# Output projection, first half: a third pair of k tiles by seven block products, and another order of the k tiles

## The chip, the cores and the metric

The kernel runs on one core of a Trainium2 chip. The engines of a core work side by side, each through its own instructions in order: TensorE (PE; its weight loads are listed as PEld), VectorE (DVE), ScalarE (ACT), GpSimd (POOL), and SyncE (SP), which issues most DMAs. The metric is the device time of one execution in microseconds (us); of several runs the median is given.

## The reference

One layer of an encoder block on 256 tokens of width 2048, in float32. Only the output projection is touched. A state-space mixer gives 1024 columns, a pooling mixer the other 1024; they are joined and multiplied by one matrix:

```python
y_ssd = ssd_mixer(z, xbc, dt_raw, ...)
y_pool = pool_mixer(u, pool_w[i], pool_scale[i])
mix = jnp.concatenate([y_ssd, y_pool], axis=-1) @ w_out[i]
h = h + rmsnorm(mix, mix_norm_post[i])
```

`w_out` has 2048 x 2048 elements. A gated feed-forward layer and a per-layer embedding follow.

## The kernel before

**Precision.** Every float32 operand is split into a rounded high part (`hi`, cast by ACT) and the rest (`lo`, a subtraction on DVE), and a product is three matmuls: high by high, high by rest, rest by high. `split` (line 146) does this to weights, in tiles of the tag "w", of which there are five (`weight_pair`, line 142). Raw weights come by DMA into tiles of the tag "raw", of which there are three.

**The projection.** The 2048 input features are 16 k tiles of 128: tiles 0 to 7 are the state-space mixer's, 8 to 15 the pooling mixer's. The output columns are made in two halves of 1024. `sublayer` (line 874) calls `token_major` (line 330) for each half; it runs through the k tiles in pairs, eight steps, in the order of a list. A half has four accumulators in PSUM, `acc[t][n]`: two blocks of 128 tokens by two blocks of 512 columns. An ordinary step casts and splits two weight tiles of 1024 columns and issues 2 x 2 x 2 x 3 = 24 matmuls of 128x512.

**Seven products.** A step in `fast` takes its two k tiles as a 2 x 2 block product with seven multiplications in place of eight (`seven_products`, line 277): 7 x 3 = 21 matmuls. For it

- the weights are split in four parts: a (one block of 512 columns), b, d and c (two blocks each). a and b are blocks of the raw weights, d and c blocks of sums that `add_blocks` (line 270, four DVE additions of 128x512) makes. For the tile pairs 0 and 2 of both halves these sums were made early in the kernel and stored in DRAM (`early_add`), and are loaded again; for other pairs `add_blocks` writes them over the raw tile, after a and b were split from it;
- the activations need sums too: `Sums` (line 853) makes them (one DVE addition of 128x512, four of 128x128, a cast on ACT and a subtraction on DVE) the first time that a pair is asked for, and keeps them for the other half;
- four of the seven products have accumulators of their own (`alt`: two main banks and the two banks of the tag "misc"), the other three go to `acc`. The order of the products is a11 (part a), a12 (b), a22 (d), s4 (b), s2 (d), s1 (c), s3 (c).

After the last fast step, `combine` (line 308, one copy on ACT and eight DVE operations of 128x512) adds the four into `acc`. It is issued with the step that follows, whose matmuls go column by column; in the last step of a half they do so too.

In the first half, the list is 8, ..., 15, 0, ..., 7; steps 4 and 5 (counted from 0: tiles 0, 1 and 2, 3) are fast, step 6 (tiles 4, 5) has the combination and step 7 (tiles 6, 7) is the last. In the second half the pairs 12, 0 and 2 are fast, as steps 2, 3 and 4; the sums of the activations of 12 and the block sums of its weights are made there.

**The turns.** Tiles 0 to 7 are the state-space mixer's output y, transposed by PE in `y_turn` (line 823, eight transposes and two scaled copies, on ACT and DVE, for two tiles). A list of jobs (line 831) puts these turns behind the ordinary steps 0 to 3: none, 0, then 2 and 4, then 6. A fast step runs no jobs.

**After a half**, each accumulator is read by ACT (a square with its sum) and by DVE (a product with the gain), lines 897 and 898. The banks of the first half's `acc` and `alt` are those of the second half's.

The order of the engines' work around here is a scheduler's: it takes it from the program's order, from what is ready in its own model, and from the tiles that are free.

Of the kernel before, what the change touches and what calls it, by code (L numbers as in the profile page):

```python
# [38 lines left out]
V_MIX, V_SCW, V_SCB, V_SN, V_PS, V_FN = 0, 16, 76, 88, 96, 104  # L39
# [14 lines left out]
def build(nc, a, out):  # L54
    x = a["x"][0]

    w_dtu, w_xbc, w_z, w_out, w_up = a["w_dtu"], a["w_xbc"], a["w_z"], a["w_out_"], a["w_up"]
# [3 lines left out]
    with tile.TileContext(nc) as tc, \  # L61
# [12 lines left out]
        def page(name, dtype=F32):  # L74
            return gp.tile([P, 2048], dtype, tag="pg", bufs=13, name=name)
# [4 lines left out]
        def tiny(name, n=2):  # L80
            return sp.tile([P, n], F32, tag="tiny", bufs=40, name=name)

        def main(name):
            return [pm.tile([P, 512], F32, tag="main", name=f"{name}_{i}") for i in range(2)]
# [32 lines left out]
        def load(dst, src, ahead=False):  # L117

            with tc.issue_after(last["dma"]) if last and not ahead else nullcontext():
                return ins(nc.sync.dma_start(dst, src))  # L120
# [15 lines left out]
        def vec(i):  # L136
            return xt[0][:, i:i + 1] if i < V_SCW else vt[:, i - V_SCW:i - V_SCW + 1]
# [53 lines left out]
        def put(dst, src, scale):  # L191

            hi, lo = dst
            return (ins(nc.scalar.activation(hi, src, AF.Identity, scale=scale)),
                    ins(nc.vector.scalar_tensor_tensor(lo, src, scale, hi.bitcast(F32),  # L195
                                                       op0=ALU.mult, op1=ALU.subtract)))
# [3 lines left out]
        work = []  # L200
# [204 lines left out]
        def rms(name, parts, scale, n=1):  # L405

            base = EPS
            for i, q in enumerate(parts):
                m = tiny(f"{name}m{i}", n)
                nc.gpsimd.tensor_scalar(m, q, scale, base, op0=ALU.mult, op1=ALU.add)  # L410
                base = m
            r = tiny(f"{name}r", n)
            nc.gpsimd.tensor_tensor(r, m, mhalf[:, :n], op=ALU.pow)
            return r

        def panel_part(name, pan, src, vcol, k0, k1):

            first = None
            for k in range(k0, k1, 2):
                ps = misc(f"{name}t{k}")  # L420
                for j in range(2):
                    for t in range(2):
                        nc.tensor.transpose(ps[:, (2 * j + t) * P:(2 * j + t + 1) * P],
                                            src[t][:, (k + j) * P:(k + j + 1) * P], ident)
                for j in range(2):
                    done = put(pan(k + j), ps[:, j * L:(j + 1) * L], vec(vcol + k + j))
                    first = first or done
            return first
# [212 lines left out]
        cat = Panel.__new__(Panel)  # L641
# [106 lines left out]
        def job(f, *args):  # L748
            return lambda: f(*args)
# [73 lines left out]
        def y_turn(k):  # L823
# [4 lines left out]
                                        y[:, t * 1024 + (k + j) * P:t * 1024 + (k + j + 1) * P], ident)  # L828
            for j in range(2):
                put(cat(k + j), ps[:, j * L:(j + 1) * L], vec(V_SN + k + j))  # L830
        work.extend([[], [job(y_turn, 0)], [job(y_turn, 2), job(y_turn, 4)], [job(y_turn, 6)]])

        def gload(name, src):
            g = cp.tile([P, D], F32, tag="gain", name=name)
            load(g, src.partition_broadcast(P))
            return g
# [37 lines left out]
        def sublayer(name, w, ks, get, gain, h, vnext, panel=Panel, fast=((), ()), sums=None, at=(), row=None, then=()):  # L874

            mg = []
            sq = [[], []]
            for half in range(2):

                alt = main(f"{name}s{half}") if fast[half] and half == 0 else []  # L880
                acc = [main(f"{name}a{half}{t}") for t in range(2)]
                if fast[half]:
                    alt += main(f"{name}s{half}") if half else []
                token_major(f"{name}{half}", w, half * 1024, ks[half], get, acc, 1, fast[half], alt, sums, at if half else ())
                mg.append(page(f"{name}m{half}"))
                for t in range(2):
                    for n in range(2):
                        q = tiny(f"{name}q{t}{half}{n}", 1)
                        m = mg[half][:, t * 1024 + n * 512:t * 1024 + (n + 1) * 512]
                        junk = sp.tile([P, 512], F32, tag="junk", bufs=1, name=f"{name}j{t}{half}{n}")  # L890
                        c = slice(half * 1024 + n * 512, half * 1024 + (n + 1) * 512)
                        b = acc[t][n]
                        if row:
                            nc.scalar.activation(junk, b, AF.Square, scale=row[t], accum_out=q)
                            nc.vector.scalar_tensor_tensor(m, b, row[t], gain[:, c], op0=ALU.mult, op1=ALU.mult)
                        else:
                            nc.scalar.activation(junk, b, AF.Square, accum_out=q)
                            nc.vector.tensor_mul(m, b, gain[:, c])
                        sq[t].append(q)
            r = [rms(f"{name}{t}", sq[t], 1.0 / D) for t in range(2)]  # L900
            pan = panel(f"{name}x")
            for c in range(4):
                s = slice(c * 512, (c + 1) * 512)
                for t in range(2):
                    m = mg[c // 2][:, t * 1024 + c % 2 * 512:t * 1024 + (c % 2 + 1) * 512]
                    nc.vector.scalar_tensor_tensor(h[t][:, s], m, r[t], h[t][:, s],
                                                   op0=ALU.mult, op1=ALU.add)
                panel_part(f"{name}x", pan, h, vnext, 4 * c, 4 * c + 4)
                if c in then:
                    then[c]()  # L910
            return pan
# [15 lines left out]
        h = [page(f"h{t}") for t in range(2)]  # L927
        for t in range(2):
            load(h[t], x[t * P:(t + 1) * P, :])
        hf = sublayer("wo", w_out, (list(range(8, 16)) + list(range(8)), [8,9,10,11,12,13,0,1,2,3,14,15,4,5,6,7]), cat, gload("gmix", a["mix_norm_post"][0]), h,  # L930
                      V_FN, Pairs, ((4,5),(2,3,4)), Sums("cs", cat))


        pl = [ple(0)]
# [415 lines left out]
```

## Time and profile before

| | us |
|---|---|
| median of three runs | 1105.33 (1105.0 to 1105.36) |
| the profiled execution | 1104.6 |
| its span, first to last instruction | 1102.8 |
| output projection, first half, on PE | 195.84 to 240.81 |
| second half, on PE | 240.81 to 283.3 |

The span is the time from the first to the last instruction of the profiled execution; 1.8 us lie around it. A row of a timeline has the start in us, how long the instruction (or a row of like ones, with their count x) took, the engine, the line of the code, the operation, the tile written <- the tiles read, shapes, and in brackets how long the engine had been idle and what released it. A matmul's row lasts longer than its turn, since matmuls overlap; its cost is the distance from start to next start. The same goes, in a smaller measure, for DVE and ACT. In the names, digits of steps are left out in places: `wo_0w` is the first weight tile of an ordinary step, `wo02dw` part d of the pair 2 of half 0, `wo112aw` part a of the pair 12 of half 1, `css` and `csp` the sums of activations, `cath` and `catl` the activations' high part and rest, `yt` the turn of y, `wom` what the last product with the gain writes.

### The profile page before, as it was taken

The numbers are of one execution on the slowest core, as the hardware profiler recorded it, in microseconds if no ns is written. First come the engines' busy times: TensorE is split into PE (matmuls) and PEld (weight loads), VectorE is DVE, ScalarE is ACT, GpSimd is POOL, SyncE is SP. The second block draws the span as 40 slices with busy tenths as digits, with TensorE's granted clock in tenths as the row PEclk, the third lists the DMA queues.
The fourth block names the chain that finished last, engine by engine and source line by source line (L and its number), as shares of the span: only waits on it lengthen the run. The fifth ranks groups of instructions, "written<-read, shape, count | busy, mean of one in ns | idle before, by whom it ended". The sixth has DMA issues, their size and how long they took to land.

```text
span 1102.8 us, 16019 instructions
## 1 busy us (share of the span) xinstructions
PE 1094.5 (99%) x5946; PEld 946.5 (86%) x5946; DVE 977.1 (89%) x1372; ACT 729.0 (66%) x1067; POOL 86.5 (8%) x145
## 2 busy tenths in 40 slices
PE   9999999999999999999999999999999999999997
PEld 9999988888888888888888888888888888888886
DVE  6589998898868998889889988898999999999996
ACT  6958763566775665665756646657688878776773
POOL 0210000100100000000000000000000000051001
PEclk9999999999999999999999999999999999999998
DMA  9885248556489999989999998999999999996872
GB/s 364 358 343 191 101 180 369 209 198 240 163 362 389 390 421 357 406 340 371 382 367 381 367 390 347 400 365 422 367 409 375 368 347 395 416 379 225 315 272 76
DMA packets 57246, 361.69 MB, mean 328 GB/s; under 512 B 6352, under 2 KB 7504, under 8 KB 21200
## 3 DMA queue, kind: packets, MB, share of 16 engines
q1 hardware_dynamic: 45648, 298.71, 69.1%
q0 software_dynamic: 11088, 61.35, 14.5%
q8 instruction: 46, 0.75, 0.3%
q10 hardware_dynamic: 432, 0.62, 0.2%
q14 instruction: 32, 0.26, 0.1%
HBM read 306.65 MB, written 54.00 MB: 327 GB/s over the span
## 4 chain that ended last, share of the span: by engine, by line
PE 97%; ACT 1%; DVE 1%; issue 0%; POOL 0%; POOLq 0%
PE ga L90 22%; PE va L90 22%; PE dna L90 11%; PE woa L90 7%; PE xbc L90 5%; PE gt L90 5%; PE dns L90 4%; PE z L90 4%; PE dtu L90 4%; PE dn0s L90 2%; PE dn1s L90 2%; PE ple L90 1%; PE gts L90 1%; PE wos L90 1%; PE yd L90 1%; PE pw L90 1%
## 5 line engine op out<-in xcount | busy, mean ns | idle before, releaser
L90 PE MATMUL ga<-wox,ug_0w 128*128 128x512 f32 x704 | 130.8, 337 | 0.0
L90 PE MATMUL ga<-wox,ug_1w 128*128 128x512 f32 x704 | 130.2, 337 | 0.0
L90 PE MATMUL va<-wox,uv_1w 128*128 128x512 f32 x704 | 129.2, 336 | 0.0
L90 PE MATMUL va<-wox,uv_0w 128*128 128x512 f32 x704 | 129.2, 336 | 0.0
L90 PEld LDWEIGHTS ga<-wox,ug_0w 128*128 128x128 f32 x704 | 107.6, 188 | 14.6 <-ACT pl L919 0.2
L90 PEld LDWEIGHTS ga<-wox,ug_1w 128*128 128x128 f32 x704 | 107.5, 188 | 14.5 <-DVE wox L195 0.2
L90 PEld LDWEIGHTS va<-wox,uv_0w 128*128 128x128 f32 x704 | 107.5, 188 | 14.5
L90 PEld LDWEIGHTS va<-wox,uv_1w 128*128 128x128 f32 x704 | 107.5, 188 | 14.5
L275 DVE TENSOR_TENSOR dnb<-dnb 128x512 f32<-128x512 f32 x128 | 88.3, 690 | 3.0
L250 POOL DMA_DIRECT2D dns<-dnb x30 | 16.1, 536 | 319.4 <-DVE dnb L275 279.8
L90 PE MATMUL xbc<-hnh,xb_0w 128*128 128x256 f32 x192 | 37.9, 284 | 0.1
L90 PE MATMUL xbc<-hnh,xb_1w 128*128 128x256 f32 x192 | 37.1, 283 | 0.0
L846 ACT CAST he<-he 128x512 fp32r<-128x512 f32 x13 | 8.1, 621 | 42.7 <-DVE he L845 42.7
L988 ACT CAST hs<-hid 128x384 fp32r<-128x384 f32 (+1 forms) x44 | 23.4, 536 | 13.5 <-PE dna L90 13.2
L90 PEld LDWEIGHTS xbc<-hnh,xb_0w 128*128 128x128 f32 x192 | 30.8, 189 | 0.8 <-ACT u L571 0.3
L1068 ACT ACTIVATE fc<-gr,vt 128x256 f32<-128x256 f32 x44 | 26.1, 594 | 7.2 <-DVE gr L1061 7.2
L90 PEld LDWEIGHTS xbc<-hnh,xb_1w 128*128 128x128 f32 x192 | 30.7, 189 | 0.1
L90 PE MATMUL dna<-dn_0w,hs 128*128 128x512 f32 x108 | 28.8, 395 | 0.0
L90 PE MATMUL dna<-dn_1w,hs 128*128 128x512 f32 x108 | 28.3, 392 | 0.0
L1139 POOL DMA_DIRECT2D hd<-hsum x24 | 12.9, 539 | 192.6 <-PE dn0s L90 70.4
L989 DVE TENSOR_TENSOR hs<-hid,hs 128x384 fp32r<-128x384 f32 (+1 forms) x44 | 25.5, 584 | 2.4 <-ACT hs L988 2.4
L90 PE MATMUL xbc<-hnl,xb_1w 128*128 128x256 f32 x96 | 27.3, 284 | 0.0
(1779 smaller groups left out, 2870.2 us busy)
## 6 DMA issues: line engine op xcount, KB each, us to landing
dnb<-w_down SPq DMA_DIRECT2D x32, 1024.0 KB, 10.0
dns<-dnb POOLq DMA_DIRECT2D x30, 1024.0 KB, 6.4
hd<-hsum POOLq DMA_DIRECT2D x24, 512.0 KB, 8.4
zr<-w_z SPq DMA_DIRECT2D x8, 1024.0 KB, 4.8
dtur<-w_dtu SPq DMA_DIRECT2D x14, 528.0 KB, 8.7
hsum<-he POOLq DMA_DIRECT2D x13, 512.0 KB, 8.0
wo0r<-w_out_ SPq DMA_DIRECT2D x6, 1024.0 KB, 5.9
gtb<-w_gate SPq DMA_DIRECT2D x6, 1024.0 KB, 10.1
```

The lines of the kernel that those rows point to most:

```text
L90: last["pe"] = ins(nc.tensor.matmul(o, lhsT, rhs, start=start, stop=stop, skip_group_check=True))
L250: nc.gpsimd.dma_start(t, pg[0])
L275: nc.vector.tensor_add(s[:, i], v[:, i], a[:, b])
L846: nc.scalar.copy(o[:, :512], s[:, :512])
L988: nc.scalar.copy(t[:, :c1], hid_part(k)[:, :c1])
L989: nc.vector.tensor_sub(t[:, 512:512 + c1], hid_part(k)[:, :c1], t[:, :c1].bitcast(F32))
L1068: nc.scalar.activation(c[:, f], v[:, f], AF.Identity, bias=vec(V_FCB + 4 * s + 2 * i + f), scale=vec(w + NF))
L1139: nc.gpsimd.dma_start(o.bitcast(F32), kept[k])
```

## The change

Two lists and one set are altered; no function is.

```diff
-        work.extend([[], [job(y_turn, 0)], [job(y_turn, 2), job(y_turn, 4)], [job(y_turn, 6)]])
+        work.extend([[], [job(y_turn, 4)], [job(y_turn, 0), job(y_turn, 2)], [job(y_turn, 6)]])
...
-        hf = sublayer("wo", w_out, (list(range(8, 16)) + list(range(8)), [8,9,10,11,12,13,0,1,2,3,14,15,4,5,6,7]), cat, gload("gmix", a["mix_norm_post"][0]), h,
-                      V_FN, Pairs, ((4,5),(2,3,4)), Sums("cs", cat))
+        hf = sublayer("wo", w_out, ([8,9,10,11,14,15,4,5,0,1,2,3,12,13,6,7], [8,9,10,11,12,13,0,1,2,3,14,15,4,5,6,7]), cat, gload("gmix", a["mix_norm_post"][0]), h,
+                      V_FN, Pairs, ((4,5,6),(2,3,4)), Sums("cs", cat))
```

In the first half, the pairs now come as 8, 10, 14, 4, 0, 2, 12, 6. Steps 4, 5 and 6 (pairs 0, 2 and 12) are fast. The block sums of the weights of pair 12 were not stored for this half, so `add_blocks` makes them in the raw tile. The sums of its activations are asked for first in this half and found again in the second. The combination is issued with step 7, which is also the last of the half. The turn of tiles 4 and 5 comes behind step 1, those of 0 to 3 behind step 2.

## The prediction

> **What bounds the kernel now.** I read the page's busy shares and its chain first, then the chain and the waits of the output projection, then the timelines of the engines there.
>
> ```profile
> PE 1094.5 (99%) x5946; PEld 946.5 (86%) x5946; DVE 977.1 (89%) x1372; ACT 729.0 (66%) x1067; POOL 86.5 (8%) x145
> PE 97%; ACT 1%; DVE 1%; issue 0%; POOL 0%; POOLq 0%
> ...
> 204.70:243.40 38.70, 38.70 (x177) 31.48 (x176) 35.92 (x53) 24.44 (x37) 0.56 (x3) 1.00 0.60 230
> 224.70:229.60 4.90, 4.90 (x22) 3.94 (x21) 4.90 (x6) 4.53 (x6) 0.00 (x0) 1.00 0.57 207
> ```
>
> TensorE (PE) is on 97% of the chain that ended last, so an added or removed microsecond of PE time in this stage is one of the kernel. The two last rows are stretches of the first half (columns: PE, PEld, VectorE (DVE), ScalarE (ACT), GpSimd (POOL) busy, granted clock, DMA): PE is busy in all of the 38.7 us, but DVE is busy in 35.92 of them, and in all 4.90 us of the second block product. The DVE time that the change adds meets a full queue; ACT and DMA (60%) have room.
>
> ```profile
> 212.96 1.03 PE L827 MATMUL yt<-ident,y 128*128 128x128 f32 x8
> 224.71 0.63 PE L90 MATMUL wos<-wo02aw,cath 128*128 128x512 f32 x2
> 225.18 0.39 PE L90 MATMUL wos<-wo02aw,catl 128*128 128x512 f32 x1
> 226.81 0.86 PE L90 MATMUL woa<-wo02bw,csp 128*128 128x512 f32 x3
> 229.61 0.63 PE L90 MATMUL woa<-wo_0w,cath 128*128 128x512 f32 x2
> 235.21 0.63 PE L90 MATMUL woa<-wo_0w,cath 128*128 128x512 f32 x2
> 240.81 1.08 PE L90 MATMUL woa<-wo_0w,cath 128*128 128x512 f32 x4
> ```
>
> These are starts on PE: the pair of tiles 2 and 3 by seven products begins at 224.71, the seventh step (an ordinary pair, 24 matmuls) at 229.61, the eighth at 235.21, the second half at 240.81. An ordinary step takes 5.60 us, so a matmul 0.2333 us; 21 of them take 4.90.
>
> **The change, part by part.** *Removed from PE.* In the seventh step 24 matmuls become 21: 3 x 0.2333 = 0.70 us. PE does not pause anywhere in this stage (the starts follow each other at that pace), so this is the whole possible gain: **-0.70**.
>
> *Added and moved on DVE.* The seventh step takes tiles 12 and 13. The block sums of their weights were not stored ahead, so they are made in place in the raw tile. Of before, the second half does just this with the same tiles (wo112):
>
> ```profile
> 243.33 0.68 DVE L867 TENSOR_TENSOR css<-cath,catl 128x512 f32<-128x512 f32 x1
> 243.93 0.69 DVE L158 TENSOR_TENSOR wo112aw<-wo112r,wo112aw 128x512 fp32r<-128x512 f32 x1
> ...
> 246.48 1.41 DVE L275 TENSOR_TENSOR wo112r<-wo112r 128x512 f32<-128x512 f32 x2
> 247.81 0.68 DVE L847 TENSOR_TENSOR csp<-css,csp 128x512 fp32r<-128x512 f32 x1
> 248.41 1.41 DVE L275 TENSOR_TENSOR wo112r<-wo112r 128x512 f32<-128x512 f32 x2
> 250.99 1.23 DVE L158 TENSOR_TENSOR wo112dw<-wo112r,wo112dw 128x1024 fp32r<-128x1024 f32 x1 [1.17 <-ACT wo112dw L157]
> 252.14 1.22 DVE L158 TENSOR_TENSOR wo112cw<-wo112r,wo112cw 128x1024 fp32r<-128x1024 f32 x1
> ```
>
> ```profile
> 249.91 1.05 ACT L157 CAST wo112dw<-wo112r 128x1024 fp32r<-128x1024 f32 x1 [2.69 <-DVE wo112r L275]
> ```
>
> From start to next start, 512 columns cost DVE 0.60 us (css) and a split of 1024 1.14 (252.14 - 250.99, rounded); the four block adds (L275) cost 1.33 + 1.41 = 2.74. Seven products split 512 + 3 x 1024 columns (4.02 us), an ordinary pair 2 x 1024 (2.28). Added: 4.02 - 2.28 + 2.74 = **4.5 us of DVE**. The sums of the activations (css, csp: 0.6 + 4 x 0.2 + 0.6 = 2.1 us with small gaps) were made for these tiles in the second half; they now come before the seventh step and are found there later. That moves 2.1 us and adds none. ACT gets 1536 more columns to cast (1.6 us by 1.05 for 1024), which lies in its idle time (24.44 of 38.70 busy). DMA: the tile of 12 was loaded whole before and still is; the transfers of stored sums stay. SP issues as many loads.
>
> *The chain in the step.* The parts a and b must be split before their blocks are overwritten; then come the four adds, ACT's cast of d, DVE's rest of d. The third product (a22) needs d: it begins 6 matmuls into the step, and its second matmul, the first to read the rest, one more: 7 x 0.2333 = 1.63 us, at 229.61 + 1.63 = 231.24. In the second half this chain was done early: d at 252.22 with the step beginning at 251.90, so 1.3 us ahead. There ordinary steps, which take two weight tiles each, come ahead of it; here two steps of four tiles do, and there are five tiles:
>
> ```profile
> 224.95 1.05 ACT L157 CAST wo_0w<-wo0r 128x1024 fp32r<-128x1024 f32 x1
> ...
> 227.71 1.05 ACT L157 CAST wo_0w<-wo0r 128x1024 fp32r<-128x1024 f32 x1 [0.27 <-PE woa L90]
> ```
>
> ```profile
> 225.07 1.22 DVE L158 TENSOR_TENSOR wo02cw<-wo02t,wo02cw 128x1024 fp32r<-128x1024 f32 x1
> ```
>
> ACT's first cast for the seventh step starts at 224.95, as the first block product ends (224.71). The cast at 227.71 waited for PE: s4 of the second block product, the last reader of its b, started its three matmuls at 226.81. So tile number n waits for number n - 5. By this, a of tile 12 is cast from 224.95 and b, which waits for the a of the second block product (its last matmul is the one of 225.18, its turn over at 225.41), from about 225.6 to 226.65.
>
> *Lower end:* DVE free, b's rest until 227.9, adds until 230.6, cast of d until 231.75, rest of d until 233.0: PE waits 233.0 - 231.24 = 1.75 us. Were two adds done while ACT casts b, about 0.65 less: 1.1.
>
> *Upper end:* DVE not free. Before, the last split of the second block product began at 225.07, so DVE was through at 226.21. The change delays it, since the turn of y's tiles 0 and 1 moves behind the third step:
>
> ```profile
> 210.02 0.69 DVE L867 TENSOR_TENSOR css<-cath,catl 128x512 f32<-128x512 f32 x1
> ...
> 214.10 1.95 DVE L195 SCALAR_TENSOR_TENSOR catl<-yt,vt,cath 128x256 fp32r<-128x256 f32 x4 [0.60 <-ACT cath L194]
> ...
> 223.93 1.22 DVE L158 TENSOR_TENSOR wo02dw<-wo02t,wo02dw 128x1024 fp32r<-128x1024 f32 x1 [0.46 <-ACT wo02dw L157]
> ```
>
> The sums of tiles 0 and 1 ran from 210.02; now they can't before their turn at 212.96, so 2.1 us of DVE work moves behind 214, into a row whose one gap is that 0.46: the end of these splits moves to 226.21 + 2.1 - 0.5 = 227.8. Then a (0.60) and b (1.14) until 229.5, adds (2.74) until 232.3, cast of d until 233.4, rest of d until 234.6: PE waits 234.6 - 231.24 = **3.4 us**. This takes it that the sums of tiles 12 and 13, whose inputs are ready long before, fill the hole that opens at 210 to 214. I take the middle of 1.75 and 3.4, **2.5 us**, as PE can bring s4 (three matmuls of b, 0.70 us) forward, and DVE some adds.
>
> Behind the waiting a22 stand PE's 14 other matmuls of the step and the whole eighth step, so nothing covers this. Behind the rest of d on DVE stand c and the eighth step's splits; c is needed 2.1 us after a22 starts over and takes 1.14, so no second wait.
>
> *The combination* (8 DVE operations of 0.6) follows the eighth step now; before, it ran under the seventh and eighth, and the read-out needed only the last matmuls:
>
> ```profile
> 237.53 0.69 DVE L898 TENSOR_TENSOR wom<-woa,gmix 128x512 f32<-128x512 f32 x1 [0.49 <-ACT woj L897]
> ```
>
> The eighth step goes column by column, so each part is combined and read out (ACT then DVE, about 1.4 us) as its six matmuls end, 1.4 us apart. The second half's first matmuls go to banks of products that are read early; its seventh matmul, 1.4 us after its start, needs the first read-out, which should be 2 us ahead of it. DVE's work from the eighth step's start until then is 4.8 + 1.2 + 1.1 = 7.1 us in about 7.0: bounds 0 and 1 us, I take 0 since only the two first read-outs must be done. In the second half DVE then lacks the 2.1 us of sums, so it catches up.
>
> *The turns.* Tiles 4 and 5 are turned a step earlier than they were; they need y's last scaling, and have it:
>
> ```profile
> 204.75 0.88 DVE L820 TENSOR_SCALAR y<-y,yn1r 128x512 f32<-128x512 f32 x2 [1.38 <-POOL yn1r L817]
> 206.97 0.60 PE L827 MATMUL yt<-ident,y 128*128 128x128 f32 x4
> ```
>
> 205.63 against 206.97: nothing. There are as many transposes, and this turn lies a whole step (5.60) ahead of the fourth step, which reads it.
>
> **Sum:** -0.70 + 2.5 = **+1.8 us**. Against the profiled execution (1104.6 with a span of 1102.8) that is 1106.4. The median of the runs, 1105.33, is 0.7 above that execution, so my time is 1105.33 + 1.8 = **1107.1**.
>
> **The rivals.** (1) *The sums of 12 do not fill the hole.* They stand behind those of 2 in the program; if DVE takes them there, 2.1 us more stand ahead of a22's weights, of which the 1.1 us of waiting for ACT's cast can hide half: waits of 4.5 to 5.5, so +3.8 to +4.8, about **1109.5**, slower. It decides where css of tile 12 stands: before 214 or after 217. For it, before, DVE idled for 1.38 us ahead of 204.75 and did not take these sums there; against it: there they stood some 40 us further on (243.33), here under 20.
> (2) *No wait.* The weights' chain is taken out of PE's way, by another order of PE's or DVE's work: -0.7, **1104.6**. For it: work of different steps does mix on PE; transposes of the next norm stand amid the ple products:
>
> ```profile
> 286.58 0.38 PE L423 MATMUL woxt<-ident,h 128*128 128x128 f32 x2
> 286.72 0.48 PE L90 MATMUL ple<-ple_0w,ptl 128*128 128x512 f32 x1
> ```
>
> Against it: DVE has no free time before, and the five tiles hold the splits back.
>
> (3) *The clock falls in the wait.* The only pause at the end:
>
> ```profile
> 1094.00:1096.00 2.00, 0.75 (x2) 0.00 (x0) 0.85 (x2) 0.97 (x3) 1.21 (x3) 1.00 0.00 0
> 1096.00:1098.00 2.00, 1.36 (x2) 0.30 (x2) 1.81 (x4) 0.40 (x1) 0.15 (x1) 0.82 0.19 65
> 1098.00:1100.00 2.00, 0.12 (x1) 0.00 (x0) 0.39 (x1) 0.59 (x1) 0.00 (x0) 0.50 0.92 324
> ```
>
> The granted clock (third column from the end) is 1.00 until 1096, 0.82 over the next 2 us and 0.50 then: it fell about 1097.3, some 2.5 us after the last dense matmuls (1094.75). A wait of that size could halve the clock. No row shows how soon it comes back: nothing lost, or, with the 5.5 us of half clock at the end as the nearest row, 2.75; with the forecast up to +4.6, **1109.9**.
> [...]
> (4) *Something else moves:* an order of work elsewhere, by over 2.2 us either way.
>
> **Chances.** About 0.2% (2.2 us) is what a measurement tells from no change. Forecast, waits of 1.1 to 3.4, +0.4 to +2.7: 0.50, of it 0.08 over 2.2. Rival 1: 0.22; 2: 0.17; 3: 0.06; 4: 0.05 (0.03 faster, 0.02 slower). Slower 0.08 + 0.22 + 0.06 + 0.02 = 0.38, same 0.42 + 0.17 = 0.59, faster 0.03. The range takes in rival 2 below and most of rival 1 above: 1104.5 to 1109.8; the likeliest case alone: 1105.7 to 1108.0.
>
> **What would show it.** Right: a pause of PE after the second product of tiles 12 and 13, released by DVE's rest of d or ACT's cast; DVE without gaps from 214 until then; css of tile 12 before 214; the second half beginning 1.8 us later. Wrong: the seventh step 4.9 us long without a pause (rival 2); a longer pause with these sums in front of it (1); a clock under 1.00 there (3); a wait at the second half's start (the combination priced too low).

## The result, and the profile after

| | before | after |
|---|---|---|
| median of five runs, us | 1105.33 (1104.91 to 1105.96) | 1111.13 (1110.33 to 1111.99) |
| ratio, with its 95% interval | | 1.0051 (1.0040 to 1.0062) |
| the profiled execution, us | 1104.6, span 1102.8 | 1111.13, span 1109.4 |
| output projection on PE, us | 195.84 to 283.31: 87.47 | 196.39 to 289.08: 92.69 |

The change made the kernel slower by 5.8 us, three times the 1.8 that was forecast, and past the upper end of the range. The spans differ by 6.6 us: 5.22 of them lie between the first matmul of the projection and the first one behind it, 0.55 ahead of it and 0.8 behind, each less than the 1.05 between the fastest and the slowest run of before. So the 5.22 us are to be found.

The page of after, busy times and the chain that ended last:

```profile
PE 1097.9 (99%) x5943; PEld 947.4 (85%) x5943; DVE 981.3 (88%) x1378; ACT 729.5 (66%) x1069; POOL 84.3 (8%) x145
...
PE 95%; DVE 2%; ACT 1%; DMA 1%; issue 1%; POOL 0%; POOLq 0%; DVEq 0%; ACTq 0%; SPq 0%
```

PE has the three matmuls less (5943 against 5946) and is busy 3.4 us longer; that alone says that its matmuls went slower somewhere. By the rows below, 1.87 of it lie in the projection (89.34 against 87.47 us busy). DVE's total rose by 4.2 us, about the 4.5 that were worked out. On the chain PE fell from 97% to 95%: the end is now set in places by DVE (2%) and DMA (1%).

The same four stretches of the projection before and after: steps 0 to 3, the two old pairs by seven products (steps 4 and 5), the last two steps, and the second half. The columns are the length, then busy time and instructions of PE, PEld, DVE, ACT and POOL, the granted clock, the DMA share and GB/s. Before:

```profile
195.84:219.74 23.90, 23.90 (x115) 19.63 (x114) 20.20 (x35) 13.26 (x22) 3.75 (x8) 1.00 0.62 241
219.74:229.61 9.87, 9.87 (x46) 7.97 (x43) 9.34 (x12) 8.69 (x11) 0.00 (x0) 1.00 0.34 115
229.61:240.81 11.20, 11.20 (x50) 9.02 (x48) 10.54 (x14) 5.68 (x11) 0.54 (x2) 1.00 0.52 189
240.81:283.31 42.50, 42.50 (x184) 34.36 (x183) 36.60 (x46) 24.84 (x33) 1.58 (x6) 1.00 0.70 258
```

After:

```profile
196.39:220.29 23.90, 23.90 (x114) 19.62 (x114) 18.18 (x33) 10.62 (x18) 3.77 (x8) 1.00 0.56 204
220.29:234.09 13.80, 11.79 (x45) 8.84 (x44) 12.79 (x21) 9.01 (x12) 0.00 (x0) 0.88 0.37 142
234.09:245.52 11.43, 10.99 (x46) 8.29 (x45) 10.23 (x13) 8.23 (x11) 0.19 (x1) 1.00 0.48 176
245.52:289.08 43.56, 42.66 (x185) 34.16 (x183) 39.23 (x46) 25.32 (x36) 1.83 (x6) 1.00 0.69 256
```

The lengths differ by 0.00, +3.93, +0.23 and +1.06: together 5.22. Most of the loss is in steps 4 and 5, which the change leaves as they were; the step that was altered is in the third row and hardly longer. The first row points to the reason: in the same 23.90 us DVE did 2.02 us less and ACT 2.64 us less than before. The hole that the later turn opens was left empty, and its work came behind 220. PE's rows in these stretches of after:

```profile
221.76 0.87 PE L90 MATMUL woa<-wo00bw,csp 128*128 128x512 f32 x3
224.52 0.50 PE L90 MATMUL woa<-wo00dw,cath 128*128 128x512 f32 x1 [1.89 <-ACT wo00dw L157]
...
236.58 0.50 PE L90 MATMUL woa<-wo012dw,cath 128*128 128x512 f32 x1 [0.22 <-ACT wo012dw L157]
...
237.53 0.50 PE L90 MATMUL wos<-wo012cw,csp 128*128 128x512 f32 x1 [0.22 <-ACT wo012cw L157]
...
250.69 0.73 PE L90 MATMUL woa<-wo_1w,cath 128*128 128x512 f32 x2 [0.90 <-DVE wo_1w L158]
```

The pause stands ahead of part d of tiles 0 and 1, the first pair by seven products. The turn of b's three matmuls is over at 221.76 + 0.70 = 222.46, and d is there at 224.52. The step of tiles 12 and 13, for which 1.1 to 3.4 us of waiting were forecast, waits only 0.22 twice: the splits had the time of the earlier pause to catch up. DVE before the pause:

```profile
212.08 1.23 DVE L158 TENSOR_TENSOR wo00bw<-wo00r,wo00bw 128x1024 fp32r<-128x1024 f32 x1 [1.54 <-ACT wo00bw L157]
214.66 1.96 DVE L195 SCALAR_TENSOR_TENSOR catl<-yt,vt,cath 128x256 fp32r<-128x256 f32 x4 [1.35 <-ACT cath L194]
216.53 1.28 DVE L867 TENSOR_TENSOR css<-cath,catl 128x512 f32<-128x512 f32 x2
...
219.15 0.68 DVE L867 TENSOR_TENSOR css<-cath,catl 128x512 f32<-128x512 f32 x1
...
222.59 0.28 DVE L845 TENSOR_TENSOR css<-css 128x128 f32<-128x128 f32 x1
223.56 0.69 DVE L847 TENSOR_TENSOR csp<-css,csp 128x512 fp32r<-128x512 f32 x1 [0.69 <-ACT csp L846]
224.50 1.23 DVE L158 TENSOR_TENSOR wo00dw<-wo00t,wo00dw 128x1024 fp32r<-128x1024 f32 x1 [0.25 <-ACT wo00dw L157]
```

And ACT:

```profile
222.91 0.62 ACT L846 CAST csp<-css 128x512 fp32r<-128x512 f32 x1 [0.76 <-DVE css L845]
223.43 1.04 ACT L157 CAST wo00dw<-wo00t 128x1024 fp32r<-128x1024 f32 x1
```

The css of 216.53 are those of the pairs 0 and 2; the third, at 219.15, is that of pair 12 (it is the one that goes when e1 below holds the sums of 12 back). It reads the pooling mixer's activations, and its inputs were ready long before; e3 below starts it at 201.43. DVE stood idle for 1.54 and 1.35 us in the hole (ahead of 212.08 and 214.66) and took this sum after both. Its last small addition is at 222.59, its cast on ACT at 222.91, and the cast of d of pair 0 stands behind that one: it starts at 223.43, though ACT had been idle for 0.76 us just before 222.91. PE's first use of d follows this cast. So a sum that is needed a pair of steps later held up a part that was needed at 222.46. The load that d's cast reads, `wo00t`, was issued at 213.76 and took 6.9 us, so it was there from 220.7. The page's chain names another releaser here, the load of pair 2's stored sums, `wo02t`, which landed at 223.12 (its 1% of DMA). The cast doesn't read that one, and in e1 the same cast started at 221.33, ahead of that load's landing at 222.6.

The rest of the 3.93 us is the clock. Windows of after, the granted clock third from the end:

```profile
224.00:225.00 1.00, 0.48 (x2) 0.30 (x2) 0.75 (x2) 1.00 (x2) 0.00 (x0) 1.00 0.00 0
225.00:228.00 3.00, 2.88 (x8) 2.05 (x7) 3.00 (x4) 2.83 (x4) 0.00 (x0) 0.50 0.00 0
228.00:229.00 1.00, 1.00 (x4) 0.78 (x4) 1.00 (x2) 0.56 (x1) 0.00 (x0) 0.79 0.00 0
```

It is halved from 225.0, just as work comes back, to about 228.42 (a mean of 0.79 is 0.42 us at half and the rest full): 3.42 us at half, by the granted clock 1.71 lost; the matmuls of 226.06, 226.49 and 226.92 start 0.43 us apart, against the 0.233 of an ordinary step before. PE's 222.46 to 224.52 is 2.06. Together 3.77 of 3.93.

### The profile page after: what moved, and what is told of

It reads as the page before. It is cut to its first block, busy times and chain, and to the rows that moved or that the text cites. A ratio compares the mean times of both kernels' runs of the same rounds, so it can differ in the third digit from the quotient of the medians.

```text
span 1109.4 us, 16020 instructions
## 1 busy us (share of the span) xinstructions
PE 1097.9 (99%) x5943; PEld 947.4 (85%) x5943; DVE 981.3 (88%) x1378; ACT 729.5 (66%) x1069; POOL 84.3 (8%) x145
## 4 chain that ended last, share of the span: by engine, by line
PE 95%; DVE 2%; ACT 1%; DMA 1%; issue 1%; POOL 0%; POOLq 0%; DVEq 0%; ACTq 0%; SPq 0%
PE ga L90 22%; PE va L90 22%; PE dna L90 11%; PE xbc L90 5%; PE gt L90 5%; PE woa L90 5%; PE dns L90 4%; PE dtu L90 4%; PE z L90 4%; PE dn0s L90 2%; PE dn1s L90 2%; PE ple L90 1%; DMA wo02t<-wos 1%; PE gts L90 1%; PE wos L90 1%; PE yd L90 1%
## 5 line engine op out<-in xcount | busy, mean ns | idle before, releaser
L988 ACT CAST hs<-hid 128x384 fp32r<-128x384 f32 (+1 forms) x44 | 23.5, 537 | 13.7 <-PE dna L90 13.4
```

Source lines behind the costliest of these rows:

```text
L988: nc.scalar.copy(t[:, :c1], hid_part(k)[:, :c1])
```

## The experiments

Eleven kernels tell the suspects apart: where the sums of pair 12 stand, the third product, the order of the pairs, the combination in the last step, DVE's time as such, and the turn. The expectations name their theories by letters: P and Q differ over what the place of these sums costs, T blames the later turn and loads, R and V differ over what is left once the sums are early, and L blames one load. The length is the projection's on PE in the profiled execution of each, less the 87.47 us of before; "before" is its median on the same chip. A length is that of a single execution: e5's took 1105.78 us, 1.5 less than its median.

| run | what it is | median, us | before, us | ratio (95%) | length |
|---|---|---|---|---|---|
| after | three fast pairs 0, 2, 12 | 1111.13 | 1105.33 | 1.0051 (1.0040 to 1.0062) | +5.22 |
| e1 | sums of 12 held back behind pair 2's splits | 1111.43 | 1105.91 | 1.0065 (1.0052 to 1.0078) | +6.89 |
| e2 | after's order, fast pairs 0 and 2 only | 1106.29 | 1105.91 | 1.0007 (0.9998 to 1.0015) | +0.82 |
| e3 | sums of 12 behind step 1 | 1109.76 | 1105.91 | 1.0040 (1.0028 to 1.0052) | +3.42 |
| e4 | fast pairs 0, 2; combination last | 1108.46 | 1105.91 | 1.0036 (1.0021 to 1.0050) | +2.55 |
| e5 | fast pairs 12, 0, 2; combination last | 1107.25 | 1105.90 | 1.0012 (1.0004 to 1.0021) | +1.86 |
| e7 | e3, block sums of 12 stored ahead | 1108.75 | 1105.90 | 1.0025 (1.0012 to 1.0038) | +2.07 |
| e8 | 12, 0, 2 fast, two ordinary steps behind | 1110.94 | 1105.90 | 1.0054 (1.0039 to 1.0070) | +5.03 |
| e9 | e2 and four DVE additions that nobody reads | 1107.25 | 1105.90 | 1.0017 (1.0009 to 1.0026) | +1.78 |
| e10 | e8, stored sums loaded earlier | 1105.93 | 1105.72 | 1.0002 (0.9994 to 1.0011) | +0.82 |
| e11 | e2, turn of tiles 0 and 1 a step earlier | 1105.90 | 1105.72 | 0.9999 (0.9990 to 1.0008) | -0.01 |
| e12 | e10, turn of 4 and 5 amid step 2 | 1106.28 | 1106.33 | 0.9998 (0.9986 to 1.0009) | +0.84 |

**e1: the sums held back.** The sums of pair 12 are put behind the splits of pair 2 on ACT and DVE.

```diff
-                    seven_products(f"{name}{k0}", name[:2], w, k0, c0, sums(k0), acc, alt, u == fast[0], u == fast[-1])
+                    with ExitStack() as behind:
+                        if (name, k0) == ("wo0", 12):
+                            for e in ("act", "dve"):
+                                behind.enter_context(tc.issue_after(last[e]))
+                        made = sums(k0)
+                    seven_products(f"{name}{k0}", name[:2], w, k0, c0, made, acc, alt, u == fast[0], u == fast[-1])
```

> The changed kernel, with the activation sums of tiles 12 and 13 put behind the last weight split of the second block product on ACT and DVE. Theory Q (these sums stand ahead of the cast of part d of pair 0 on ACT and DVE, PE waits 1.9 us, the clock falls for 3.4 us): no pause of PE in step 4 and a clock of 1.00 there, about 3 to 4 us won, 1106 to 1108. Theory T (the later turn of tiles 0 and 1, and the later loads of the stored sums, make the pause): the pause stays, 1110 to 1112. Theory P (the 4.5 us of DVE work of the third product are what is lost, wherever they stand): the pause moves to step 6 with its size, 1109 to 1111.

PE's rows with a wait in e1, steps 4 and 6:

```profile
222.41 0.50 PE L90 MATMUL woa<-wo00dw,cath 128*128 128x512 f32 x1 [0.44 <-ACT wo00dw L157]
...
233.90 0.50 PE L90 MATMUL woa<-wo012bw,csp 128*128 128x512 f32 x1 [0.45 <-DVE csp L852]
...
236.36 0.58 PE L90 MATMUL woa<-wo012dw,cath 128*128 128x512 f32 x1 [1.96 <-ACT wo012dw L157]
```

The wait for d in step 4 fell from 1.89 to 0.44, as in e2 below: the sums ahead of d were its cause. But nothing was won: as theory P had it, there is a pause in step 6 instead, 0.45 for the sums and 1.96 for d, and the clock was halved there for 3.42 us. The wait for d in step 6 isn't the late sums' doing: e3 below has one of 1.90 with the sums early. It is the third pair's own chain, which had been covered by the earlier pause in after.

**e2: the order alone.** The new order and turns, but pair 12 as an ordinary step.

```diff
-                      V_FN, Pairs, ((4,5,6),(2,3,4)), Sums("cs", cat))
+                      V_FN, Pairs, ((4,5),(2,3,4)), Sums("cs", cat))
```

> The new order of the k tiles and of the turns, with two fast steps as before (pair 12 is an ordinary step 6). Q and P: no pause, 1104.5 to 1106 (the same as before). T: a pause in step 4 with a fall of the clock, 1108 to 1110.

PE's rows with a wait in e2:

```profile
223.02 0.50 PE L90 MATMUL woa<-wo00dw,cath 128*128 128x512 f32 x1 [0.43 <-ACT wo00dw L157]
...
223.97 0.50 PE L90 MATMUL wos<-wo00cw,csp 128*128 128x512 f32 x1 [0.21 <-ACT wo00cw L157]
```

The new order and turns cost 0.82 us by themselves (the ratio's interval takes in 1), 0.64 of it these two waits for pair 0's d and c. That is near what Q and P expected (1104.5 to 1106), and not T's 1108 to 1110. The other 4.4 us of after come with the third pair, by which the combination moves to the last step.

**e3: the sums early.** The forecast had assumed that these sums stand in the hole. Here they are made as a job behind step 1.

```diff
-        work.extend([[], [job(y_turn, 4)], [job(y_turn, 0), job(y_turn, 2)], [job(y_turn, 6)]])
+        cs = []
+        work.extend([[], [job(y_turn, 4), lambda: cs[0](12)], [job(y_turn, 0), job(y_turn, 2)], [job(y_turn, 6)]])
...
+        cs.append(Sums("cs", cat))
...
-                      V_FN, Pairs, ((4,5,6),(2,3,4)), Sums("cs", cat))
+                      V_FN, Pairs, ((4,5,6),(2,3,4)), cs[0])
```

> The changed kernel, with the activation sums of tiles 12 and 13 asked for right behind the turn of tiles 4 and 5, after step 1, where DVE had an idle stretch of about 3 us (210 to 214.7). Q: no pause in step 4, and less work behind 214 than in the kernel with the sums put behind: 1104.5 to 1107. T: pause in step 4 stays, 1109 to 1111. P: about 1108 to 1110, waits in step 6 and at the second half's start.

DVE in e3 ends the sums of pair 12 in time:

```profile
210.63 0.69 DVE L848 TENSOR_TENSOR csp<-css,csp 128x512 fp32r<-128x512 f32 x1
```

PE's rows with a wait in e3, and two windows from the pause on:

```profile
234.40 0.50 PE L90 MATMUL woa<-wo012dw,cath 128*128 128x512 f32 x1 [1.90 <-ACT wo012dw L157]
...
235.35 0.50 PE L90 MATMUL wos<-wo012cw,csp 128*128 128x512 f32 x1 [0.22 <-ACT wo012cw L157]
...
248.51 0.73 PE L90 MATMUL woa<-wo_1w,cath 128*128 128x512 f32 x2 [0.89 <-DVE wo_1w L158]
```

```profile
234.40:236.00 1.60, 1.38 (x5) 0.86 (x6) 1.60 (x2) 1.60 (x2) 0.00 (x0) 1.00 0.02 5
236.00:238.00 2.00, 2.00 (x11) 1.62 (x10) 2.00 (x3) 2.00 (x3) 0.00 (x0) 1.00 0.21 33
```

The rows show no wait in step 4, and the pause is where the forecast had put it: after b of tiles 12 and 13, released by ACT's cast of d. The first half takes 47.05 us (196.26 to 243.31) against 44.97 before, +2.08; with the 0.70 of the matmuls put back, 2.78 were lost, 2.12 of them in these two waits. The clock did not fall in this execution (1.00 in both windows), though the pause is as long as in after. The time is the one that theory P expected (1108 to 1110), not Q's (1104.5 to 1107): in this order of the pairs, the third pair's chain costs its pause with early sums too. The second half took 43.84 us, 1.34 more than before, the last of these waits among it.

**e4 and e5: the combination in the last step.** Both take the pairs as 8, 10, 14, 4, 12, 0, 2, 6 in the first half, so the combination is issued with the last step, as in after. In e4 pair 12 is ordinary, as before; in e5 it is fast, with two fast pairs behind it. This is e4's edit; e5 has the same list, and its fast steps stay 4, 5 and 6.

```diff
-        hf = sublayer("wo", w_out, ([8,9,10,11,14,15,4,5,0,1,2,3,12,13,6,7], ...
-                      V_FN, Pairs, ((4,5,6),(2,3,4)), Sums("cs", cat))
+        hf = sublayer("wo", w_out, ([8,9,10,11,14,15,4,5,12,13,0,1,2,3,6,7], ...
+                      V_FN, Pairs, ((5,6),(2,3,4)), Sums("cs", cat))
```

> Two fast steps only (pairs 0 and 2), but as steps 5 and 6, with the ordinary pair 12 as step 4 ahead of them: the combination is issued with the half's last step, as in the change, and no third product is made. If the combination in the last step costs, PE waits in the first step of the second half (0.9 us there in the changed kernel): 1106 to 1107.5. If that wait came from DVE being late with the third product: none, 1104.5 to 1105.8.

> Three fast steps as in the change, but pair 12 first: steps 4, 5, 6 are the pairs 12, 0, 2, so ordinary steps stand ahead of the in-place sums, and the activation sums of 12 stand ahead of everything that hangs on y. Theory R (three separate costs: the wait for part d of pair 12, about 2; the combination in the last step, about 1 to 1.5; the sums of 12 ahead of the cast for pair 0): the wait for d goes, the one at the second half's start stays at 0.9, 1105.5 to 1107.5. Theory V (the total of VectorE's work is what counts, wherever it stands): 1108 to 1110.

The wait at the second half's start in e4:

```profile
246.84 0.72 PE L90 MATMUL woa<-wo_1w,cath 128*128 128x512 f32 x2 [0.88 <-DVE wo_1w L158]
```

The same wait is there in after (0.90), e1 (0.87), e3 (0.89), e4 (0.88), e5 (0.91) and e7 (0.89), and in none of e2, e8, e9, e10, e11 and e12, whose combination has another step behind it. It needs no third product: e4 has two fast pairs, as before, and is still 2.55 us longer, 1.89 of it in the second half, where pair 12's d and c wait too (0.28 and 0.23); 1106 to 1107.5 were expected. DVE around it, in after:

```profile
246.43 0.68 DVE L898 TENSOR_TENSOR wom<-woa,gmix 128x512 f32<-128x512 f32 x1
247.03 0.69 DVE L328 TENSOR_TENSOR woa<-woa,wo0v 128x512 f32<-128x512 f32 x1
247.62 1.88 DVE L898 TENSOR_TENSOR wom<-woa,gmix 128x512 f32<-128x512 f32 x3
249.42 1.22 DVE L158 TENSOR_TENSOR wo_1w<-wo1r,wo_1w 128x1024 fp32r<-128x1024 f32 x1
```

The end of the combination and all four read-outs (L898) stand without a gap ahead of the rest of a weight tile that PE wants. The second half is longer than before by 0.65 us in e7, 1.06 in after, 1.07 in e1, 1.34 in e3 and e5 and 1.89 in e4, the wait included. With pair 12 first, DVE makes its sums early unasked, in e5 from 206.88 to 212.1:

```profile
206.88 0.68 DVE L867 TENSOR_TENSOR css<-cath,catl 128x512 f32<-128x512 f32 x1
```

PE then waits only 0.23 and 0.22 in the first half, which is 0.52 us longer than before (196.02 to 241.51): the wait for d of pair 12 is gone and the one at the second half's start stays, as theory R had it. Of the kernels with three fast pairs and the combination last, e5 is the fastest, at 1.0012, and still slower than before.

**e7: the block sums stored ahead.** e3, and the block sums of pair 12's weights are made early in the kernel and stored, as those of 0 and 2 are.

```diff
+        work[1].append(job(early_fetch, 0, 12))
+        work[3].append(job(early_add, 0, 12))
```

> The kernel with the activation sums of 12 early, and the block sums of the weights of pair 12 of the first half made and stored during the z projection, as those of pairs 0 and 2 are; the four adds (2.7 us) leave the half. R: the wait of 1.9 in step 6 goes, the 0.9 at the second half's start stays: 1106 to 1107.5. V: both shrink, as VectorE has 2.7 us less: 1105 to 1106.5.

PE's rows with a wait in e7, first half:

```profile
224.35 0.73 PE L90 MATMUL woa<-wo00bw,csp 128*128 128x512 f32 x2 [1.00 <-ACT csp L849]
...
225.90 0.50 PE L90 MATMUL woa<-wo00bw,csp 128*128 128x512 f32 x1 [0.82 <-DVE csp L850]
```

The wait of step 6 is gone, which fits the chain through the raw tile as its cause, but does not show it: 1.82 us turned up in step 4, for the sums of pair 0's activations, and a pause there had covered the wait of step 6 in after too. The 0.89 at the second half's start stayed. The stage also begins later than in the others (197.12 against 195.74 to 196.48); that the early additions make this is likely, but not shown. Neither R (1106 to 1107.5) nor V (1105 to 1106.5) had the time.

**e8 and e10: two ordinary steps behind.** Pairs 12, 0 and 2 are fast as steps 3 to 5; 4 and 6 follow, and the combination lies under an ordinary step again.

```diff
-        work.extend([[], [job(y_turn, 4)], [job(y_turn, 0), job(y_turn, 2)], [job(y_turn, 6)]])
+        work.extend([[], [job(y_turn, 0), job(y_turn, 2)], [job(y_turn, 4), job(y_turn, 6)]])
...
-        hf = sublayer("wo", w_out, ([8,9,10,11,14,15,4,5,0,1,2,3,12,13,6,7], ...
-                      V_FN, Pairs, ((4,5,6),(2,3,4)), Sums("cs", cat))
+        hf = sublayer("wo", w_out, ([8,9,10,11,14,15,12,13,0,1,2,3,4,5,6,7], ...
+                      V_FN, Pairs, ((3,4,5),(2,3,4)), Sums("cs", cat))
```

> Three fast steps, 3, 4 and 5 (pairs 12, 0, 2), with two ordinary steps (4, 6) behind them, so that the combination lies under step 6 as before the change; turns of 0 and 2 after step 1, of 4 and 6 after step 2. R: no wait but small ones, 0.7 us of matmuls gained: 1104.5 to 1106. V: VectorE as loaded as in the change, waits of 2 to 4 us: 1107.5 to 1109.5.

The wait at the second half's start is gone in e8, but there is a pause of 2.50 us in pair 2, and the clock falls behind it (half from 230.84 to 234.26, 3.42 us again; the matmuls of 232.17 and 232.60 start 0.43 us apart, those from 234.52 on 0.233). The 1110.94 are neither R's (1104.5 to 1106) nor V's (1107.5 to 1109.5). ACT in e8:

```profile
229.22 1.04 ACT L157 CAST wo02dw<-wo02t 128x1024 fp32r<-128x1024 f32 x1 [2.39 <-DMA wo02t<-wos]
```

And SP's queue:

```profile
217.68 4.47 SPq L120 DMA_DIRECT2D wo0r<-w_out_  x2
...
222.24 0.38 SPq L120 DMA_DIRECT2D wo02t<-wos  x1
```

The stored sums of pair 2 (`wo02t`) were issued at 222.24 and took 6.9 us to land, behind two raw loads that held SP until raw tiles came free: it waited 13.4 us ahead of the first, for DVE's split of c of pair 12, and 3.8 between the two. e10 issues both loads of stored sums behind step 1, ahead of these raw loads:

```diff
+        def stored_back(k):
+            r = page(f"wot{k}")
+            last["dma"] = load(r, sums_["wo", 0, k][0], True)
+            sums_["wo", 0, k] = r, True
-        work.extend([[], [job(y_turn, 0), job(y_turn, 2)], [job(y_turn, 4), job(y_turn, 6)]])
+        work.extend([[], [job(y_turn, 0), job(y_turn, 2), job(stored_back, 0), job(stored_back, 2)], [job(y_turn, 4), job(y_turn, 6)]])
```

> Three fast steps 3, 4, 5 (pairs 12, 0, 2) with the combination under step 6, as in the run where PE waited 2.5 us for the stored block sums of pair 2 (their load stood behind a load that waited for a raw tile, and landed at 229). Here both loads of stored sums are issued after step 1, ahead of that. If that load was what this order cost (theory L): no pause over 0.6, clock 1.00, 1105 to 1106.5. If VectorE's added work is the cost in this order too (theory V): pauses of 1.5 to 3 us in other places, 1107.5 to 1110.

PE's rows with a wait in e10:

```profile
219.32 0.93 PE L90 MATMUL wo0s<-wo012dw,csp 128*128 128x512 f32 x3 [0.79 <-DVE catl L195]
...
227.28 0.50 PE L90 MATMUL woa<-wo_0w,cath 128*128 128x512 f32 x1 [0.32 <-ACT wo_0w L157]
```

From e8's 1110.94 to 1105.93, level with before (1.0002), as theory L had it: the load's place in the queue was the cause, and 4.2 us of the projection hung on it, the clock's fall among them. What is left is the 0.70 us of the matmuls against 1.11 us of waits and 0.41 that no wait shows. 0.79 of the waits is for a bank of the tag "misc" that a turn of y still occupies: DVE's `catl` frees it.

**e9: DVE time as such.** e2, with the four additions of 128x512 for pair 12 into a page that nothing reads.

```diff
+                if (name, k0) == ("wo0", 12):
+                    add_blocks(r, page("unread"))
```

> The order of the change with two fast steps, and in step 6 the four block adds of pair 12 (2.7 us of VectorE) into a page that nobody reads: VectorE's time without anyone who waits for its result. R: at most 0.5 us more than the order alone, which stood at 1106.3. V: 1.5 to 2.7 more, 1107.8 to 1109, with PE waiting for splits behind the adds.

DVE in e9, and then PE's wait:

```profile
220.91 0.68 DVE L275 TENSOR_TENSOR unread<-wo0r 128x512 f32<-128x512 f32 x1
...
221.94 0.68 DVE L275 TENSOR_TENSOR unread<-wo0r 128x512 f32<-128x512 f32 x1
222.54 1.41 DVE L275 TENSOR_TENSOR unread<-wo0r,unread 128x512 f32<-128x512 f32 x2
223.87 1.22 DVE L158 TENSOR_TENSOR wo00dw<-wo00t,wo00dw 128x1024 fp32r<-128x1024 f32 x1
```

```profile
225.14 0.50 PE L90 MATMUL woa<-wo00dw,cath 128*128 128x512 f32 x1 [0.96 <-DVE wo00dw L158]
```

Additions that nobody waits for cost 0.96 us more than e2, this wait, which stands beside e2's two: DVE took all four ahead of the rest of pair 0's d. That is neither at most 0.5, as R had it, nor 1.5 to 2.7, as V had it: DVE's time in this stretch costs by what it pushes back.

**e11: the turn.** e2 with the turn of tiles 0 and 1 behind step 1 again.

```diff
-        work.extend([[], [job(y_turn, 4)], [job(y_turn, 0), job(y_turn, 2)], [job(y_turn, 6)]])
+        work.extend([[], [job(y_turn, 0), job(y_turn, 4)], [job(y_turn, 2)], [job(y_turn, 6)]])
```

> The new order of the k tiles with two fast steps (no third product), but tiles 0 and 1 are turned after step 1 together with 4 and 5, so that their sums can be made from 210 on, as before the change. If the later turn makes the waits of 0.4 and 0.2 us in step 4 of the order alone: they go, and it is 0.4 to 0.8 faster than the order alone, level with the kernel before. If the loads of the stored sums make them: they stay.

PE waits nowhere in the stage, and the length is that of before (-0.01). So the 0.82 us of e2 go with the later turn of tiles 0 and 1, and the new order of the pairs costs nothing beside it.

**e12: the turn amid a step.** e10, with the turn of tiles 4 and 5 in the middle of step 2, to be out of the bank's way.

```diff
-                for t, (o, c), (k, wh, wl), q in order:
+                for n_, (t, (o, c), (k, wh, wl), q) in enumerate(order):
+                    if (name, k0, n_) == ("wo0", 14, 12):
+                        mid_turn[0](4)
...
-        work.extend([[], [job(y_turn, 0), job(y_turn, 2), job(stored_back, 0), job(stored_back, 2)], [job(y_turn, 4), job(y_turn, 6)]])
+        work.extend([[], [job(y_turn, 0), job(y_turn, 2), job(stored_back, 0), job(stored_back, 2)], [job(y_turn, 6)]])
```

> The run with three fast steps 3, 4, 5, the combination under step 6 and the stored sums loaded early, and the turn of tiles 4 and 5 moved from the end of step 2 into its middle, as PE waited 0.79 us there for DVE to empty the bank of that turn. If that wait goes without another in its place, the output projection from its first matmul to the first of the embedding takes 87.2 to 87.8 us (before 87.47, without this move 88.29) and the kernel 1105.0 to 1105.8, level with before or up to 0.3 better. If DVE is simply late there, the wait comes back at the next split: 88 to 88.6, 1105.9 as without it.

The wait for the bank only moved, as the expectation had it if DVE is simply late: PE's transposes now wait for DVE themselves.

```profile
212.32 0.63 PE L830 MATMUL yt<-ident,y 128*128 128x128 f32 x4 [1.20 <-DVE catl L195]
```

Level with before once more (0.9998). No version beat before.

## Why the prediction was wrong

**Right.** The gain of at most 0.70 us; the 4.5 us of added DVE time (4.2 in the page's totals); DVE as what a third pair runs into; the turn of tiles 4 and 5 for nothing (e11 has it, and no wait). The chain of the weights of pair 12 was also right in place, mechanism and size, under its own assumption: e3, where the assumption holds, shows 1.90 + 0.22 us of waits and 2.78 us lost in the first half, with 2.5 forecast from bounds of 1.1 and 3.4. Of its signs of being wrong, a clock under 1.00, a wait at the second half's start and css of 12 after 217 all came.

**The steps that failed** are three: where the sums of tiles 12 and 13 stand, the combination at 0, and the clock kept out of the sum. The first is the sentence "This takes it that the sums of tiles 12 and 13, whose inputs are ready long before, fill the hole that opens at 210 to 214." They did not, and DVE idled there for 2.9 us. Rival 1 named the case and the row that decides it (css of 12 before 214 or after 217: it was at 219.15). But it added the delay to the wait of the altered step. It struck two steps earlier, where no rival had looked: the cast of the sums stands on ACT and waits for DVE, and the cast of pair 0's d, ready, stands behind it. Asking what is behind the waiting instruction on its engine was done for PE and DVE, and not for ACT, which looked free with 24.44 of 38.70 us busy.

In time, this step is worth less than it looks. The pause moved: 1.89 us in step 4 of after, 1.90 in step 6 of e3, where the sums stand as assumed. That the 2.06 us on PE are near the 2.5 of the forecast is luck, since they come from another wait. Of the 1.80 us between after's 5.22 and e3's 3.42, 1.71 are the clock, from which e3's profiled execution was spared. And with the assumption true, e3 still took 3.85 us more than before (1109.76 against 1105.91), where 1.8 were forecast.

So the size of the miss lies in the other two steps. The projection lost 3.42 us more than the 1.8: 1.71 for the clock, 1.06 for the second half, which the sum had at 0, and 0.65 as the waits and small losses of the first half came to 3.15 in place of 2.5.

**The sign that misled.** "The seventh step 4.9 us long without a pause" was to show rival 2, no wait. The step came nearly so, with 0.22 twice, and meant the opposite: the pause had been taken two steps earlier. Such a sign needs the length of the stage beside it.

**The clock.** Rival 3 had the right mechanism and a fair price: the row at the kernel's end gave 0 to 2.75 us, and the 3.42 us at half that were measured make 1.71. But it stood beside the sum with a chance of 0.06, as a rival to the others, when it follows from any of them: a pause of 2 us comes first, whichever cause it has. Of the four kernels with one pause of 1.89 us or more, three lost the clock (after, e1, e8) and one did not (e3). Rival 1's 1109.5 with these 1.71 on top would have been near the 1111.13 measured, though by other terms: it has the wait in step 6 and no combination.

**The combination.** It was taken at 0 from bounds of 0 and 1 us, "since only the two first read-outs must be done". DVE did all four ahead of the split, and the wait is 0.87 to 0.91 us in each of six kernels. The second half lost 1.06 us in after and 0.65 to 1.89 in the other five. The reckoning beside it, 7.1 us of work in 7.0, was the warning: it had two read-outs in it, and the other two add 1.2. From the combination's first operation on DVE in after, at 241.10, to the split at 249.42 it is 8.3 us without a gap. With no slack, the order decides, and the value to take was the upper bound. "In the second half DVE then lacks the 2.1 us of sums, so it catches up" did not help, since PE had waited by then.

**The later turn** of tiles 0 and 1 was counted only as work in front of pair 12's chain. By e2 and e11 it costs 0.8 us of its own, in step 4, without a third product; e3 has the later turn too, and its rows show no wait there, so that this price hangs on the order of the work around it.

The sum by the measured terms: -0.70 for the matmuls, 2.06 for the pause and 1.71 for the clock, 0.93 for the waits and small losses of steps 6 and 7 and 0.16 of steps 4 and 5, 1.06 for the second half: 5.22. The range missed the time since it joined the rivals as alternatives; two of them and the upper bound of the combination came together.

**Left open.** Why the order on DVE and ACT puts the sums of pair 12 behind those of 2, when their inputs are there before, the runs don't show. Why the clock fell in after and not in e3, whose pause is as long, they don't show either; e3 has one trace. What the combination costs beyond the wait of 0.9 us (e4's second half lost 1.89) wasn't taken apart.

## What to carry to other kernels

Where an engine is fed by one that is nearly full, saving 0.7 us of matmuls by adding 4.5 us to the feeder has little to win: of the eight kernels here with a third pair, six were slower (1.0012 to 1.0065), and the two whose order and loads had been placed by hand (e10, e12) were level. An idle stretch need not fill itself because an input is ready (after: DVE idle for 2.9 us ahead of the sums of pair 12). Count what stands behind a waiting instruction on every engine and on the load queue, those that look idle too: here a ready cast behind another (after, 1.9 us) and a load behind others that waited for their tiles (e8, 2.5 us) each made a pause behind which the clock was halved. And rivals that follow from each other, such as a pause and the clock that falls in it, are priced together.

## What the runs showed of the hardware

**A pause of 1.89 us halved the clock in one run, and one of 1.90 left it alone in another.** In after the clock fell at 225.0, 2.5 us after the turn of the last dense matmul was over (222.46), two matmuls after a pause of 1.89 us; in e3 a pause of 1.90 us in the same pattern left it at 1.00. These are single executions. Where it fell it stayed at half for 3.42 us, in after, e1 and e8 alike (e1's windows):

```profile
236.00:237.00 1.00, 0.64 (x2) 0.30 (x2) 0.66 (x1) 1.00 (x2) 0.00 (x0) 0.82 0.00 0
237.00:240.00 3.00, 3.00 (x7) 2.15 (x7) 3.00 (x4) 3.00 (x4) 0.00 (x0) 0.50 0.11 19
240.00:241.00 1.00, 1.00 (x6) 0.79 (x5) 1.00 (x2) 0.85 (x2) 0.00 (x0) 0.97 0.74 229
```

0.36 us at half in the first row, 3.00 and 0.06: 3.42, of which half, 1.71 us, counts as lost by the granted clock. No run here shifts a pause by itself, so what decides whether the clock falls is not shown.
